# Seven block products in place of eight in the gelu half of two up-projections

## The chip, the cores and the metric

The kernel runs on one core of a Trainium2 chip. The metric is device time in microseconds (us) of one execution, and smaller is better. The core has a matrix engine (TensorE, PE in the profile; its weight loads are listed as PEld), a vector engine (VectorE, DVE), a scalar engine for activation functions and copies (ScalarE, ACT), a general engine (GpSimd, POOL) and an engine that mostly issues transfers (SyncE, SP). Each engine works through its own queue in order, and they meet by semaphores. Matmul results go to eight banks of an accumulator memory, each of 128 partitions by 512 fp32 columns; all other tiles lie in on-chip memory or in DRAM.

## The reference

Two decoder layers on x of 512 tokens by 1024 features: layer 0 mixes tokens by dilated attention, layer 1 by a gated linear recurrence, and each is followed by a gated convolutional feed-forward network. The change touches the feed-forward networks alone:

```python
def causal_dwconv(x, w, b):
    K = w.shape[0]
    S = x.shape[1]
    xp = jnp.pad(x, ((0, 0), (K - 1, 0), (0, 0)))
    out = b
    for k in range(K):
        out = out + xp[:, k:k + S] * w[k]
    return out

def conv_ffn(x, w_up, conv_w, conv_b, w_down):
    u = causal_dwconv(x @ w_up, conv_w, conv_b)
    g, v = u[..., :D_FF], u[..., D_FF:]
    return (jax.nn.gelu(g, approximate=True) * v) @ w_down
```

D_FF is 3072, the convolution has three taps along the tokens, and `x @ w_up` is 512 x 1024 by 1024 x 6144. Its first 3072 columns go through gelu (the gelu half), the others are multiplied onto them (the value half).

## The kernel before, in words

**Precision.** Matmuls take the fast fp32 format, which keeps fewer bits. So each operand is held as a rounded part hi and a remainder lo, and each product is three matmuls: hi by hi, hi by lo, lo by hi (`mm3`, L257, and `PASSES`, L255). `split` (L148) makes the two parts of a weight tile: ScalarE copies into hi (L149), VectorE subtracts hi from the raw tile into lo (L150).

**Activations.** A layer's normalized input lies transposed in two tiles hT (hi and lo), 128 partitions by 8 feature blocks by 512 tokens.

**Weights.** All weights are read in chunks of 1 MB in the order of the list `plan`. For an up-projection the plan alternates for j = 0 to 11: a gelu chunk (256 columns of the gelu half, all 1024 rows), then the value chunk with the same j. `load` (L193) issues a chunk's transfer on SyncE's queue into one of three raw buffers (RAW_BUFS). `parts_of` (L157) cuts a chunk into two units of 128 columns, and `pump` (L167) splits one unit per step into hi and lo, in two cuts of 512 columns each, as long as fewer than eight units live (W_UNITS). It asks for more chunks only when no cut piece is left over. `take` hands a unit to the matmuls, `done` gives it back, and `tick` (L222), called after each tile of matmuls, moves the side work on by a step and pumps one or two units. So the order on every engine follows from the places of these calls in the program: nothing is scheduled later.

**The up-projection.** `ffn` (L591) runs j = 0 to 11 and calls `feat_tiles(2, hT, ...)` (L433). For each of the two chunks and each of its two units it takes a bank and lets `feat` (L423) run 8 feature blocks by 3 passes, 24 matmuls of 128 x 128 weights by 512 tokens. Pair j = 0 runs in two halves of 256 tokens, since the last tokens' normalization comes late. After each tile the `sink` (L607) is issued: `conv` (L594) has ScalarE scale and bias the bank into a tile u (L596) and VectorE add the two other taps from the bank (L600, 511 and 510 columns). Gelu tiles (b = 0, 1) then go through gelu on ScalarE (L611) and stay until the down-projection; value tiles (b = 2, 3) are multiplied onto the gelu tiles by VectorE (L615).

**The rest.** `rows_proj` (L458) is the down-projection with the post-norm, which adds onto the residual x, held in `x_sb` (128 x 4 x 1024 fp32) for the whole program. Two `gain` buffers (128 x 1024) hold norm gains, and a pool of 32 tiles of 128 x 512 (`gen`) holds everything else. GpSimd's queue issues transfers of the attention, of gains and of transposed tiles; while an up-projection runs it has nothing to do.

## Time and profile before

| | |
|---|---|
| median time of 3 runs | 1455.94 us (1455.89 to 1456.03) |
| span of the profiled execution, first to last instruction | 1454.0 us (the page gives no time of its own for it) |
| mean granted TensorE clock | 0.999 |
| chain from pair 0 to the end of layer 0's up-projection | 1176 matmuls, 510.5 to 764.3 us |
| moved by transfers | 172.76 MB, mean 119 GB/s |

The profile is one execution. Busy time of an engine is the union of its instructions; a group row gives, for one line, engine and shape, the busy time, the mean length of one instruction in ns, and the idle time just before them with what ended it. Matmuls are pipelined: a row may say 390 ns for a matmul while the next starts after 227, so pitches are taken from long stretches and not from lengths. The chain that ended last is followed back from the last instruction through what released each step. A row of the windows gives, for a stretch, its length and then busy time and number of instructions of PE, PEld, DVE, ACT and POOL, then the granted clock, the transfers' share and GB/s.

### The profile page before, as it was taken

The numbers are of one execution on the slowest core, as the hardware profiler recorded it, in microseconds if no ns is written. First come the engines' busy times: TensorE is split into PE (matmuls) and PEld (weight loads), VectorE is DVE, ScalarE is ACT, GpSimd is POOL, SyncE is SP. The second block draws the span as 40 slices with busy tenths as digits, with TensorE's granted clock in tenths as the row PEclk, the third lists the DMA queues.
The fourth block names the chain that finished last, engine by engine and source line by source line (L and its number), as shares of the span: only waits on it lengthen the run. The fifth ranks groups of instructions, "written<-read, shape, count | busy, mean of one in ns | idle before, by whom it ended". The sixth has DMA issues, their size and how long they took to land.

```text
span 1454.0 us, 18793 instructions
## 1 busy us (share of the span) xinstructions
PE 1445.0 (99%) x6861; PEld 1214.4 (84%) x6861; DVE 879.8 (61%) x1955; ACT 675.9 (46%) x1532; POOL 133.9 (9%) x275
## 2 busy tenths in 40 slices
PE   9999999999999999999999999999999999999998
PEld 7888888888888898888888888888898888888886
DVE  6767747474735975555564338769775555564333
ACT  7656636262615553343444335589453434444221
POOL 0340414040402100000000001000100000000000
PEclk9999999999999999999999999999999999999999
DMA  7653637372726343323323322432333233223201
GB/s 225 207 146 109 174 113 208 104 215 97 216 96 211 102 131 100 103 87 102 101 88 116 115 73 88 131 116 84 120 102 116 87 102 102 87 104 128 88 0 58
DMA packets 125364, 172.76 MB, mean 119 GB/s; under 512 B 8736, under 2 KB 102392, under 8 KB 125272
## 3 DMA queue, kind: packets, MB, share of 16 engines
q1 hardware_dynamic: 114280, 145.48, 31.0%
q0 software_dynamic: 10144, 25.04, 5.9%
q8 instruction: 54, 0.88, 0.2%
q10 hardware_dynamic: 848, 1.05, 0.2%
q14 instruction: 38, 0.31, 0.1%
HBM read 156.24 MB, written 15.29 MB: 118 GB/s over the span
## 4 chain that ended last, share of the span: by engine, by line
PE 93%; ACT 4%; DVE 3%; issue 1%; DVEq 0%; ACTq 0%
PE ps L259 55%; PE acc L259 24%; PE v L758 8%; PE v L688 1%; DVE xb L967 1%; PE O L909 1%; PE S L854 1%; PE S L808 1%; DVE wlo L150 1%; ACT sig L988 1%; ACT whi L149 1%; PE O L259 1%; PE tr L341 1%; ACT sig L1007 0%; ACT a L1005 0%
## 5 line engine op out<-in xcount | busy, mean ns | idle before, releaser
L259 PE MATMUL ps<-hT,whi 128*128 128x512 f32 (+1 forms) x2752 | 801.3, 375 | 0.0
L259 PEld LDWEIGHTS ps<-hT,whi 128*128 128x128 f32 x2752 | 503.6, 188 | 91.6
L259 PE MATMUL ps<-hT,wlo 128*128 128x512 f32 (+1 forms) x1376 | 515.3, 374 | 0.0
L150 DVE TENSOR_TENSOR wlo<-raw,whi 128x512 fp32r<-128x512 f32 x360 | 230.8, 686 | 187.2 <-ACT whi L149 187.1
L259 PEld LDWEIGHTS ps<-hT,wlo 128*128 128x128 f32 x1376 | 259.1, 188 | 46.5
L149 ACT ACTIVATE whi<-raw 128x512 fp32r<-128x512 f32 x360 | 204.6, 621 | 135.4 <-PE acc L259 121.0
L600 DVE SCALAR_TENSOR_TENSOR u<-ps,cols,u 128x511 f32<-128x511 f32 x192 | 143.8, 749 | 140.6 <-ACT u L596 137.2
L259 PE MATMUL acc<-whi,ahi 128*128 128x512 f32 x512 | 199.7, 390 | 0.0
L259 PE MATMUL acc<-whi,alo 128*128 128x512 f32 x512 | 199.4, 389 | 0.1
L259 PE MATMUL acc<-wlo,ahi 128*128 128x512 f32 x512 | 199.3, 389 | 0.0
L143 ACT ACTIVATE whi<-raw,first_w 128x128 fp32r<-128x128 f32 (+1 forms) x432 | 146.2, 425 | 56.6 <-PE ps L259 33.9
L596 ACT ACTIVATE u<-ps,cols 128x512 f32<-128x512 f32 x96 | 74.8, 779 | 210.0 <-PE ps L259 210.0
L144 DVE SCALAR_TENSOR_TENSOR wlo<-raw,first_w,whi 128x128 fp32r<-128x128 f32 (+1 forms) x432 | 139.5, 389 | 1.4 <-ACT whi L143 1.3
L259 PEld LDWEIGHTS acc<-whi,alo 128*128 128x128 f32 x512 | 96.1, 188 | 20.5 <-DVE alo L150 0.5
L259 PEld LDWEIGHTS acc<-whi,ahi 128*128 128x128 f32 x512 | 96.1, 188 | 19.8
L259 PEld LDWEIGHTS acc<-wlo,ahi 128*128 128x128 f32 x512 | 96.2, 188 | 19.8
L758 PE MATMUL v<-whi,hT 128*128 128x512 f32 x320 | 102.4, 393 | 0.0
L302 POOL DMA_DIRECT2D turned<-T x36 | 19.6, 547 | 763.4 <-DVE T L296 759.9
L309 POOL DMA_DIRECT2D ft<-turned x144 | 78.7, 554 | 39.6 <-issue 17.7
L758 PEld LDWEIGHTS v<-whi,hT 128*128 128x128 f32 x320 | 60.1, 188 | 12.3
L611 ACT ACTIVATE u<-u 128x512 f32<-128x512 f32 x48 | 30.3, 632 | 80.4 <-DVE u L600 80.4
L758 PE MATMUL v<-wlo,hT 128*128 128x512 f32 x160 | 62.3, 389 | 0.0
(171 smaller groups left out, 1010.7 us busy)
## 6 DMA issues: line engine op xcount, KB each, us to landing
raw<-in_ffn_w_up_dram SPq DMA_DIRECT2D x48, 1024.0 KB
raw<-in_attn_w_qkv_dram SPq DMA_DIRECT2D x67, 512.0 KB
raw<-in_ffn_w_down_dram SPq DMA_DIRECT2D x24, 1024.0 KB
raw<-in_lru_w_in_dram SPq DMA_DIRECT2D x8, 1024.0 KB
turned<-T POOLq DMA_DIRECT2D x28, 256.0 KB, 2.6
ft<-turned POOLq DMA_DIRECT2D x112, 64.0 KB, 5.8
vrows<-v SPq DMA_DIRECT2D x16, 256.0 KB
vp<-vrows SPq DMA_DIRECT2D x16, 256.0 KB
```

The lines of the kernel that those rows point to most:

```text
L143: nc.scalar.activation(hi[:, k], raw[:, k], AF.Copy, scale=w)
L144: nc.vector.scalar_tensor_tensor(lo[:, k], raw[:, k], w, hi[:, k].bitcast(F32), op0=ALU.mult, op1=ALU.subtract)
L149: nc.scalar.activation(hi, raw, AF.Copy)
L150: nc.vector.tensor_tensor(lo, raw, hi.bitcast(F32), op=ALU.subtract)
L259: mm(dst, l[a], r[b], start=start and n == 0, stop=stop and n == 2)
L302: nc.gpsimd.dma_start(d, T)
L309: nc.gpsimd.dma_start(t[32 * c : 32 * c + 32].rearrange("j (b x) -> j b x", b=4), d.rearrange("(b j) (c x) -> c j b x", j=32, c=4)[c],)
L341: nc.tensor.transpose(ps[:, k * P : (k + 1) * P], xs[i][:, k * P : (k + 1) * P], ident)
L596: nc.scalar.activation(u, ps, AF.Identity, scale=cc[:, j : j + 1], bias=cc[:, 48 + j : 49 + j])
L600: nc.vector.scalar_tensor_tensor(u[:, d:], ps[:, : S - d], wc, u[:, d:], op0=ALU.mult, op1=ALU.add)
L611: nc.scalar.activation(u, u, AF.Gelu_apprx_tanh)
L758: mm(banks[t], hT[a][:, k, t * P : (t + 1) * P], W[b][:, k % 2, :], start=(k, a, b) == (0, 0, 0), stop=(k, a, b) == (KD - 1, 1, 0),)
```

## The change

For j = 3 to 10 in both layers (16 pairs) the gelu chunk's 256 x 1024 by 1024 x 512 product is done in 2 x 2 blocks: two halves of 128 output columns (m), two halves of 512 rows (k), two halves of 256 tokens (n). Seven block products (Strassen's scheme in Winograd's form) replace the eight, each of 4 feature blocks by 3 passes, 12 matmuls of 128 x 128 weights by 256 tokens.

*Weights* (`summed`). With a, b the two row halves of the first 128 columns and c, d of the other 128, c becomes c + d by a transfer on GpSimd's queue (`add_rows`, issued by `load` behind the chunk's own transfer), which reads d from DRAM a second time and adds it into the raw buffer. Four units follow in the raw buffer: (a, c+d); then VectorE makes a + c + d; (a + c + d, b); then VectorE makes two more sums; the third unit; and d alone. The first three are split in one piece of 1024 columns, d in one of 512. The pieces of a pair are ordered: value unit 0, the four gelu units, value unit 1. `pump` starts on a pair when both its chunks are asked for.

*Tokens* (`token_sums`). Once per layer, as side work from pair 1 on, GpSimd adds hi and lo of hT, VectorE forms four sums of its blocks, and they are split into hi and lo. They lie in the place of `x_sb`, in both gain buffers and in four pool tiles. For that, x is copied to DRAM first and comes back at j = 11 (`x_back`); `X[0]` names the tile that holds it now.

*Products* (`seven`). Numbers 1 to 7 are products, letters a to h are quarters of the value chunk's two tiles (6 matmuls of 512 tokens each). Bank y0 gathers products 1 and 2 in columns 0 to 255, bank y1 products 5, 3, 6, 7, 4. Between them ScalarE copies product 5 and then 5 + 3 out of y1 and writes minus product 1 into it, VectorE writes a difference into the other half of y0 after product 6 and of y1 after product 7. The four sinks are issued behind 2, d, 4 and h.

The diff, without the hunks that only rename `x_sb` to `X[0]`:

```diff
@@ -36,6 +36,7 @@
 TOE_BUFS = 2
 CP_PAD = 8
 WARM = 5
+SEVEN = range(3, 11)
 
 SHORT_ORDER = [
     ([0, 1], [0, 1, 2]), ([0], [3]), ([2, 3], [0]), ([1], [3]), ([2, 3], [1]), ([2], [2, 3]), ([3], [2, 3]),
@@ -153,6 +154,44 @@
     state = {"dma": 0, "cv": 0, "live": 0, "next": 0, "hold": False}
     raws, units, pieces = {}, {}, []
     sides, first_w, first_y, one = [], [], [], []
+
+    def plain(i, j, raw):
+
+        def f(hi, lo):
+            h = raw.shape[1] // 2
+            cuts = [(slice(None), slice(0, h)), (slice(None), slice(h, 2 * h))]
+            if raw.shape[1] == 1:
+                cuts = [(slice(None), slice(0, 1), slice(n, n + 512)) for n in (0, 512)]
+            if plan[i][4] is not None:
+                split_normed(hi, lo, raw, plan[i][4] + (2 * j if plan[i][0] == "value" else 0))
+                cuts = []
+            for c in cuts:
+                split(hi[c], lo[c], raw[c])
+
+        return (i, j), list(raw.shape[1:]), f
+
+    def summed(i, raw):
+
+        a, b, c, d = (raw[:, 4 * k : 4 * k + 4, m * P : m * P + P] for m, k in ((0, 0), (0, 1), (1, 0), (1, 1)))
+        shape = [KD, P]
+
+        def first(hi, lo):
+            two = [h.rearrange("p (k m) c -> p k (m c)", m=2) for h in (hi, lo)]
+            split(*two, raw[:, 0:4, :])
+            nc.vector.tensor_tensor(a, a, c, op=ALU.add)
+
+        def second(hi, lo):
+            split(hi, lo, raw[:, :, 0:P])
+            nc.vector.tensor_tensor(b, a, b, op=ALU.add)
+            nc.vector.tensor_tensor(a, a, d, op=ALU.subtract)
+
+        def third(hi, lo):
+            split(hi, lo, raw[:, :, 0:P])
+
+        def fourth(hi, lo):
+            split(hi[:, 0:4], lo[:, 0:4], d)
+
+        return [((i, n), shape, f) for n, f in enumerate((first, second, third, fourth))]
 
     def parts_of(kind, raw):
 
@@ -168,24 +207,21 @@
 
         for _ in range(limit):
             i = state["cv"]
-            if not pieces and i < state["dma"]:
-                pieces.extend((i, j, u) for j, u in enumerate(parts_of(plan[i][0], raws.pop(i))))
-                state["cv"] += 1
+            if not pieces and i + (i < len(plan) and plan[i][0] == "wino") < state["dma"]:
+                if plan[i][0] == "wino":
+                    u, v = summed(i, raws.pop(i)), [
+                        plain(i + 1, j, r) for j, r in enumerate(parts_of("feat", raws.pop(i + 1)))
+                    ]
+                    pieces.extend([v[0], *u, v[1]])
+                    state["cv"] += 2
+                else:
+                    pieces.extend(plain(i, j, r) for j, r in enumerate(parts_of(plan[i][0], raws.pop(i))))
+                    state["cv"] += 1
             if pieces and state["live"] < W_UNITS:
-                i, j, raw = pieces.pop(0)
-                hi, lo = (
-                    wp.tile([P] + list(raw.shape[1:]), F32R, tag=t, name=nm("w" + t)) for t in ("hi", "lo")
-                )
-                h = raw.shape[1] // 2
-                cuts = [(slice(None), slice(0, h)), (slice(None), slice(h, 2 * h))]
-                if raw.shape[1] == 1:
-                    cuts = [(slice(None), slice(0, 1), slice(n, n + 512)) for n in (0, 512)]
-                if plan[i][4] is not None:
-                    split_normed(hi, lo, raw, plan[i][4] + (2 * j if plan[i][0] == "value" else 0))
-                    cuts = []
-                for c in cuts:
-                    split(hi[c], lo[c], raw[c])
-                units[i, j] = (hi, lo)
+                key, shape, fill = pieces.pop(0)
+                hi, lo = (wp.tile([P] + shape, F32R, tag=t, name=nm("w" + t)) for t in ("hi", "lo"))
+                fill(hi, lo)
+                units[key] = (hi, lo)
                 state["live"] += 1
             while not pieces and state["dma"] < len(plan) and state["dma"] - state["cv"] < RAW_BUFS:
                 load()
@@ -198,8 +234,13 @@
         for src, n in srcs:
             nc.sync.dma_start(raw[:, :, at : at + n] if kind == "value" else raw[:, at : at + n, :], src)
             at += n
+        if kind == "wino":
+            add_rows(raw[:, 0:4, P:256], srcs[0][0][:, 4:8, P:256])
         raws[i] = raw
         state["dma"] += 1
+
+    def add_rows(to, src):
+        nc.gpsimd.dma_start(to, src, accum_op=ALU.add)
 
     def chunk():
         i = state["next"]
@@ -234,12 +275,12 @@
         while sides:
             tick()
 
-    def w_cols(w, c0, normed=False):
+    def w_cols(w, c0, normed=False, kind="feat"):
         if normed:
             srcs = [(w[i * 512 : (i + 1) * 512, c0 : c0 + 256].rearrange("(p k) c -> p k c", k=4), 4) for i in range(2)]
         else:
             srcs = [(w[:, c0 : c0 + 256].rearrange("(k p) c -> p k c", p=P), KD)]
-        plan.append(("feat", KD, 256, srcs, 0 if normed else None))
+        plan.append((kind, KD, 256, srcs, 0 if normed else None))
 
     def w_value(w, *cuts):
 
@@ -617,11 +658,140 @@
         order = [([0, 1, 2, 3], range(9)), ([0], range(9, 12)), ([1], range(9, 12))]
         order += [([2, 3], [9]), ([2], [10, 11]), ([3], [10, 11])]
         prep, run = rows_proj(12, act_split(gv), order, post, pre)
+        T = []
         for j in range(12):
+            if j == 1:
+                side(token_sums(hT, T))
             if j == 11:
+                x_back()
                 prep(3)
-            feat_tiles(2, hT, lambda b, ps: sink(b, ps, j), j == 0)
+            if j in SEVEN:
+                seven(hT, T, lambda b, ps: sink(b, ps, j))
+            else:
+                feat_tiles(2, hT, lambda b, ps: sink(b, ps, j), j == 0)
         return run()
+
+    kept = []
+
+    def x_back():
+
+        X[0] = cp.tile([P, 4, D], F32, tag="x_sb", name=nm("x_sb"))
+        nc.gpsimd.dma_start(X[0], kept.pop())
+
+    def token_sums(hT, T):
+
+        assert len(sides) == 1
+        d = dp.tile([P, 4, D], F32, name=nm("x_kept"))
+        nc.gpsimd.dma_start(d, X[0])
+        kept.append(d)
+        homes = cp.tile([P, 4, D], F32R, tag="x_sb", name=nm("T"))
+        homes = [homes[:, n] for n in range(4)]
+        homes += [cp.tile([P, D], F32R, tag="gain", name=nm("T"), bufs=2) for _ in range(2)]
+        homes = [[h[:, 0:512], h[:, 512:1024]] for h in homes]
+        homes += [[gen(F32R, "T") for _ in range(2)] for _ in range(2)]
+        homes = [[h.rearrange("p (k t) -> p k t", k=2) for h in hs] for hs in homes]
+        yield 1
+
+        def both(k0, n):
+            o = gen(s="B").rearrange("p (k t) -> p k t", k=2)
+            hi, lo = (h[:, k0 : k0 + 2, n * 256 : n * 256 + 256] for h in hT)
+            nc.gpsimd.tensor_tensor(o, hi.bitcast(F32), lo.bitcast(F32), op=ALU.add)
+            return o
+
+        tt = nc.vector.tensor_tensor
+        B = {}
+        for k in range(2):
+            for n, at in (((0, 0), 2 * k), ((0, 1), 2 * k), ((1, 1), 4 + 2 * k), ((1, 0), 4 + 2 * k)):
+                B[k, n] = both(at, n[1])
+        yield 2
+        for k in range(2):
+            b11, b12, b22, b21 = (B[k, n] for n in ((0, 0), (0, 1), (1, 1), (1, 0)))
+            tt(b11, b11, b12, op=ALU.subtract)
+            tt(b12, b12, b22, op=ALU.subtract)
+            tt(b22, b22, b11, op=ALU.add)
+            tt(b21, b21, b22, op=ALU.subtract)
+            yield 1
+            for n, b in enumerate((b11, b22, b12, b21)):
+                split(homes[2 * n][k], homes[2 * n + 1][k], b)
+            if not k:
+                yield 1
+        T.extend([homes[2 * n], homes[2 * n + 1]] for n in range(4))
+
+    def seven(hT, T, sink):
+
+        i, iv = chunk(), chunk()
+        t = gen(s="part")
+        y, v = {}, {}
+
+        def block(kr, n):
+            return lambda h, k: hT[h][:, 4 * kr + k, n * 256 : n * 256 + 256]
+
+        def turn(n):
+            return lambda h, k: T[n][h][k // 2][:, k % 2]
+
+        def pairs(m):
+            return lambda w, k: w.rearrange("p (k m) c -> p k m c", m=2)[:, k, m]
+
+        def row(k0):
+            return lambda w, k: w[:, k0 + k]
+
+        left = {
+            1: (0, pairs(0), block(0, 0), 0), 5: (0, pairs(1), turn(0), 1), 6: (1, row(0), turn(1), 1),
+            2: (1, row(4), block(1, 0), 0), 7: (2, row(0), turn(2), 1), 3: (2, row(4), block(1, 1), 1),
+            4: (3, row(0), turn(3), 1),
+        }
+
+        def product(n):
+            u, l, r, b = left[n]
+            W = take(i, u)
+            if b not in y:
+                y[b] = psum()
+            for k in range(4):
+                for q, (wa, ha) in enumerate(PASSES):
+                    mm(
+                        y[b][:, 0:256], l(W[wa], k), r(ha, k), start=n in (1, 5) and k == q == 0,
+                        stop=k == 3 and q == 2, skip_group_check=True,
+                    )
+
+        def quarter(n):
+            m, k0 = n // 4, 2 * (n % 4)
+            W = take(iv, m)
+            if m not in v:
+                v[m] = psum()
+            for k in (k0, k0 + 1):
+                mm3(v[m], [w[:, k, :] for w in W], [h[:, k, :] for h in hT], k == 0, k == KD - 1)
+
+        a, c = (lambda: y[0][:, 0:256]), (lambda: y[1][:, 0:256])
+        p5, z = t[:, 0:256], t[:, 256:512]
+        for step in "5a13bc62d7ef4gh":
+            if step in "1234567":
+                n = int(step)
+                product(n)
+                if n == 5:
+                    nc.scalar.activation(p5, c(), AF.Copy)
+                elif n == 1:
+                    done()
+                elif n == 3:
+                    nc.scalar.activation(z, c(), AF.Copy)
+                    nc.scalar.activation(c(), a(), AF.Copy, scale=-1.0)
+                elif n == 6:
+                    nc.vector.tensor_tensor(y[0][:, 256:512], z, c(), op=ALU.subtract)
+                elif n == 2:
+                    done()
+                    sink(0, y[0])
+                elif n == 7:
+                    done()
+                    nc.vector.tensor_tensor(y[1][:, 256:512], c(), p5, op=ALU.subtract)
+                else:
+                    done()
+                    sink(1, y[1])
+            else:
+                n = "abcdefgh".index(step)
+                quarter(n)
+                if n % 4 == 3:
+                    done()
+                    sink(2 + n // 4, v[n // 4])
+            tick()
 
 
     def attention(hT, post, pre):
@@ -1072,7 +1242,7 @@
             for c in range(4):
                 w_rows(lru_w_out[0], c * 256)
         for j in range(12):
-            w_cols(ffn_w_up[layer], j * 256)
+            w_cols(ffn_w_up[layer], j * 256, kind="wino" if j in SEVEN else "feat")
             w_cols(ffn_w_up[layer], D_FF + j * 256)
         for c in range(12):
             w_rows(ffn_w_down[layer], c * 256)
```

More of the change, by code (lines that the diff above doesn't have):

```diff
@@ L130 @@
     make_identity(nc, ident)
-    x_sb = cp.tile([P, 4, D], F32, tag="x_sb", name="x_sb")
+    X = [cp.tile([P, 4, D], F32, tag="x_sb", name="x_sb")]
     def gain(src, layer, eng=nc.gpsimd):
@@ L315, in prenorm @@
     def prenorm(t, hT, g, wait):
-        xh, gh = halves(x_sb[:, t, :]), halves(g)
+        xh, gh = halves(X[0][:, t, :]), halves(g)
         xs = [gen(s="xs") for _ in range(2)]
@@ L353, in first_transposed @@
                 ps[:, k % 4 * P : (k % 4 + 1) * P],
-                x_sb[:, t, i * 512 : i * 512 + 512].rearrange("t (p k) -> t k p", k=4)[:, k % 4], ident,
+                X[0][:, t, i * 512 : i * 512 + 512].rearrange("t (p k) -> t k p", k=4)[:, k % 4], ident,
             )
@@ L375, in first_squares @@
             nc.scalar.activation(
-                junk, x_sb[:, t, i * 512 : i * 512 + 512], AF.Square, accum_out=first_ss[i][:, t : t + 1]
+                junk, X[0][:, t, i * 512 : i * 512 + 512], AF.Square, accum_out=first_ss[i][:, t : t + 1]
             )
@@ L409, in postnorm @@
         for i, c in enumerate(at):
-            xc = x_sb[:, t, c]
+            xc = X[0][:, t, c]
             nc.vector.scalar_tensor_tensor(xc, u[i], y, xc, op0=ALU.mult, op1=ALU.add)
@@ L1090, in x_half @@
         c = slice(i * 512, (i + 1) * 512)
-        nc.sync.dma_start(x_sb[:, t, c], x[0, t * P : (t + 1) * P, c])
+        nc.sync.dma_start(X[0][:, t, c], x[0, t * P : (t + 1) * P, c])
     def w_part(i, k0, k1):
```

## The prediction

> **What bounds the kernel now.** First the page's list of engines, then the share of the chain that ended last:
>
> ```profile
> span 1454.0 us, 18793 instructions
> PE 1445.0 (99%) x6861; PEld 1214.4 (84%) x6861; DVE 879.8 (61%) x1955; ACT 675.9 (46%) x1532; POOL 133.9 (9%) x275
> PE 93%; ACT 4%; DVE 3%; issue 1%; DVEq 0%; ACTq 0%
> ```
>
> TensorE is busy for 99% of the span and carries 93% of the chain, so a cheaper set of matmuls is the right place to look. How close it runs shows in the chain in order of time, asked from 495 to 900 us (start, length, what); that stretch holds all of layer 0's up-projection:
>
> ```profile
> 500.13 5.75 PE ps L259 x48
> 510.50 253.77 PE ps L259 x1176
> 764.27 125.12 PE acc L259 x552
> ```
>
> The first row is 48 matmuls of 256 columns (the halves of pair 0): 5.75/48 = 0.1198 us each. The last is 552 of 512 columns: 0.2267 us each. Between them 1176 matmuls run with nothing else in the chain: in the up-projection TensorE waits for nobody. A pair j (gelu chunk and value chunk, 96 matmuls of 512) lasts 96 x 0.2267 = 21.76 us. What the other engines do meanwhile, over eight pairs (busy time and count by engine):
>
> ```profile
> 568.00:742.00 174.00, 174.00 (x769) 144.12 (x769) 98.98 (x144) 68.41 (x112) 0.00 (x0) 1.00 0.29 97
> ```
>
> VectorE (third engine) works 12.4 us a pair, ScalarE (fourth) 8.6, GpSimd nothing. They have room, but only because nothing on TensorE hangs on them soon: a finished tile sits in its bank while 5.4 us of the next tile run, and weights are split up to eight units ahead.
>
> **What the change takes away.** A gelu chunk was 48 matmuls of 512, 48 x 0.2267 = 10.88 us. Seven products of 4 x 3 matmuls of 256 are 84 x 0.1198 = 10.06 us. So 0.82 us a pair, 16 pairs: 13.1 us, or 0.9%. The saving is so much less than one eighth because a 256-column matmul costs 53% of a 512-column one.
>
> The Trainium skill ("TensorE: Matmul & The Clock Gate", Back-to-back issue gap) gives columns/2.4 + 2.5 ns. By it the saving would be 48 x 215.8 - 84 x 109.2 ns = 1.19 us a pair, 19 us in all; the rows above are of this very work, so I go by them.
>
> **What it adds on VectorE and ScalarE.** Durations (mean ns, second number behind the bar), from the groups by line with shapes kept apart:
>
> ```profile
> L150 DVE TENSOR_TENSOR wlo<-raw,whi 128x512 fp32r<-128x512 f32 x360 | 230.8, 686 | 187.2 <-ACT whi L149 187.1
> L149 ACT ACTIVATE whi<-raw 128x512 fp32r<-128x512 f32 x360 | 204.6, 621 | 135.4 <-PE acc L259 121.0 <-PE ps L259 14.4
> L143 ACT ACTIVATE whi<-raw,first_w 128x128 fp32r<-128x128 f32 x384 | 115.2, 390 | 24.1 <-PE ps L259 24.1
> L143 ACT ACTIVATE whi<-raw,first_w 128x512 fp32r<-128x512 f32 x48 | 31.4, 713 | 32.5 <-DMA raw<-in_attn_w_qkv_dram 22.7 <-PE ps L259 9.9
> L144 DVE SCALAR_TENSOR_TENSOR wlo<-raw,first_w,whi 128x128 fp32r<-128x128 f32 x384 | 105.8, 345 | 1.3 <-ACT whi L143 1.3
> L144 DVE SCALAR_TENSOR_TENSOR wlo<-raw,first_w,whi 128x512 fp32r<-128x512 f32 x48 | 33.7, 744 | 0.1
> L596 ACT ACTIVATE u<-ps,cols 128x512 f32<-128x512 f32 x96 | 74.8, 779 | 210.0 <-PE ps L259 210.0
> L600 DVE SCALAR_TENSOR_TENSOR u<-ps,cols,u 128x511 f32<-128x511 f32 x96 | 71.9, 749 | 137.2 <-ACT u L596 137.2
> L600 DVE SCALAR_TENSOR_TENSOR u<-ps,cols,u 128x510 f32<-128x510 f32 x96 | 71.9, 749 | 3.4
> L615 DVE TENSOR_TENSOR u<-u,u 128x512 f32<-128x512 f32 x48 | 33.2, 692 | 1.6
> L611 ACT ACTIVATE u<-u 128x512 f32<-128x512 f32 x48 | 30.3, 632 | 80.4 <-DVE u L600 80.4
> ```
>
> No row has 1024 or 256 columns of this kind, so I scale. ScalarE: (713-390)/384 = 0.84 ns a column; a 1024-wide split is 0.621 + 0.43 = 1.05 us (bounds: one 512 row, 0.62, and two of them, 1.24), a 256-wide copy 0.41 (bounds 0.39 and 0.62). VectorE: (744-345)/384 = 1.04 ns a column; 1024 wide is 1.22 (0.69 to 1.37), 256 wide 0.42 (0.34 to 0.69).
>
> Per pair VectorE loses four 512 subtractions (2.74) and gains three 1024 subtractions (3.66), one of 512, three weight sums of 512 (2.74 together) and two 256 differences in the banks (0.84): 12.4 + 4.5 = 16.9 us. ScalarE loses 2.48 and gains 3.15 + 0.62 + 1.23: about 11.1. Both still fit in 21 us. As a sum, then, all of it hides. It does not hide as a chain, because TensorE now waits for these engines inside the pair. Its order is 5 a 1 3 b c 6 2 d 7 e f 4 g h; a product takes 12 x 0.1198 = 1.44 us, a value quarter 6 x 0.2267 = 1.36. Three waits are new.
>
> *Before product 4.* It adds to bank y1, from which VectorE must first have taken product 7's difference. VectorE's queue is in order, and between the end of product 2 and that difference stand: ScalarE's first tap of gelu tile 0 (0.78), two taps on VectorE (1.50), gelu (0.63, ahead of the next split on ScalarE), the third weight unit's split (1.05) and subtraction (1.22), the two taps of value tile 0 (1.50), its multiply (0.69), the fourth unit's subtraction (0.69), and the difference (0.42). Sum 8.5 us. TensorE has d, 7, e and f to cover it: 1.44 + 3 x 1.36 = 5.5. It stands for about **3.0 us**. Behind product 4 in TensorE's queue are g, h and the next pair, so nothing fills the hole. With the low bounds of the scaled items the stand is 1.9, with the high ones 3.6.
>
> *Before product 2.* VectorE's difference after product 6 goes into columns 256 to 511 of bank y0, product 2 into 0 to 255 of the same bank, with nothing between 6 and 2. If product 2 waits, it waits for the last matmul of 6 to drain, the difference (0.42), and what VectorE still has ahead (two weight sums of 0.69 each, partly beside product 6). How long a drain is:
>
> ```profile
> L259 PE MATMUL ps<-hT,whi 128*128 128x256 f32 x384 | 69.9, 284 | 0.0
> L259 PEld LDWEIGHTS ps<-hT,whi 128*128 128x128 f32 x2752 | 503.6, 188 | 91.6
> ```
>
> 0.28 us per matmul less the 0.12 pitch is 0.16; with two handovers and the difference 0.65, with a late VectorE up to 1.3. I take **0.8**. Whether it waits at all no row shows, since the kernel before never lets VectorE write a bank in use. The Trainium skill ("PSUM — Partial Sum Buffer", PSUM bank collisions raise a hardware error) says two engines must be kept apart by bank, not by address. If columns alone counted, this term would be nothing and the time 13 us shorter.
>
> *Before product 6.* ScalarE must copy y1 out and write minus product 1 into it. From the end of product 4: tap 0.78, taps 1.50, gelu 0.63, two value splits 1.24, tap of value tile 1 0.78, taps 1.50, multiply 0.69, first unit's subtraction 1.22 and sum 0.69, second unit's split 1.05, two copies 0.82: 10.9 us. TensorE has g, h, 5, a, 1, 3, b, c: 5 x 1.36 + 3 x 1.44 = 11.1. An even race: I take **0.3** (0 to 0.8).
>
> **What hides.** A gelu chunk's load is asked for a whole pair ahead (three raw buffers, a pair takes two), and the adding transfer follows it on GpSimd's queue, which is otherwise idle here. Rows for its size, last number the us from issue to landing:
>
> ```profile
> turned<-T POOLq DMA_DIRECT2D x28, 256.0 KB, 2.6
> cn<-crow POOLq DMA_DIRECT2D x8, 256.0 KB, 6.1
> gain<-in_norm_ffn_post_dram POOLq DMA_DIRECT2D x2, 512.0 KB, 4.0
> ```
>
> A load of 1 MB (some 4 to 8 us by the last row) and an addition of 2.6 to 6.1 are done 10 to 20 us before the first split wants them; beyond that each us would cost ScalarE one, in every pair. The token sums (per layer 8 sums on GpSimd, 8 on VectorE, 8 splits: 11 us of VectorE, 5 of ScalarE) fall into pairs 1 and 2, where both are idle for over a third; the first seven-product pair starts with their backlog, 2 us a layer (0 to 8, since no row has a GpSimd sum). The copy of x out and back has the whole projection and GpSimd's queue to itself: nothing. SyncE's loads go out in twos instead of singly, after the pair's last piece; they keep over half a pair of lead.
>
> **Sum.** Stands 3.0 + 0.8 + 0.3 = 4.1 a pair, less 0.82: +3.3 us, 16 pairs +52.5; backlog 2 x 2 = 4; and TensorE's restart after 48 stands, whose next weight load is no longer hidden (0.19 at most, its row's mean; say 0.04 each): 2. Together +58 on a span of 1454.0: 1512. The runs shown have a median of 1455.94, 1.9 above that span, which I carry over: **1514 us**. With all low bounds a pair gains 1.9 + 0.65 - 0.82 = 1.7 us (+28, 1484), with all high ones 3.6 + 1.3 + 0.8 - 0.82 = 4.9 and 16 of backlog (+94, 1550).
>
> **Rivals.**
> *Slower still, by late sums.* GpSimd's token sums or the adding transfers take some three times what I allow; the first pairs of each layer, or ScalarE in each pair, wait for them. For it: no row shows either operation. Against: the long lead. Some 20 us more: 1535. Chance 9%.
> *The clock falls in the stands.* The last matmul in the timeline (start, length), and the clock column (before the last two) after it:
>
> ```profile
> 1446.93 0.39 PE L259 MATMUL acc<-whi,alo 128*128 128x512 f32 x1
> ...
> 1451.00:1452.00 1.00, 0.00 (x0) 0.00 (x0) 0.00 (x0) 0.00 (x0) 0.00 (x0) 1.00 0.99 371
> 1452.00:1453.00 1.00, 0.00 (x0) 0.00 (x0) 0.00 (x0) 0.00 (x0) 0.00 (x0) 0.77 0.41 154
> ```
>
> The matmul ends at 1447.3; the clock was still whole after 4.7 us of rest. If a stand of 3 us halved it until product 5, then 4, g and h (4.16 us) would take twice that: 67 us more, 1581. Chance 3%. The Trainium skill (the TensorE page above, Part 1) wants an idle window of about 3.4 us, free-running, before the clock drops; by it a 3.0 us stand never does it, a 3.6 us one seldom.
> *Milder.* The wide operations lie at their low ends and product 2 does not wait: a pair costs 1 us: 1475. Chance 4%.
> *Not slower.* The difference before product 4 comes in time. Only if the chain from product 2 to it is at most 5.7 us instead of 8.5 (5.5 of cover, and 0.15 beside the 0.65 at product 2) do the stands eat no more than the 0.82 saved. With no stand at all the time is 1456 - 13 = 1443. For it: VectorE and ScalarE are not full. Against: eight of its ten items are rows as they stand. Chance 3%.
> *The blocks cost TensorE more.* Were 256-column products with changing weights bound by weight loads, a pair would lose; but pair 0's halves load new weights for each matmul at 0.1198. 1%, 1550.
>
> Forecast 80%, own range 1490 to 1540. The range for all, 1488 to 1550, leaves out the clock, the milder case and the gain. A measurement of this kernel can tell about 0.2% from no change: faster 3%, same 1%, slower 96%.
>
> **What would show it.** In the profile after: TensorE no longer at 99% but near 95%, products waiting for VectorE (some 3 us, then 0.8, once a pair each) with ScalarE third and small; pairs 3 to 10 lasting about 25 us instead of 21.76; a 256-column pitch near 0.12; no wait on the adding transfer; the clock whole. I would be wrong if products follow each other without gaps, if the gaps stand at DMA, or if a 1024-wide operation differs much from 1.05 and 1.22 us.

## The result and the profile after

| | before | after |
|---|---|---|
| median time | 1455.91 us (1455.77 to 1456.03, 4 runs) | 1555.55 us (1554.24 to 1556.32, 4 runs) |
| span of the profiled execution | 1454.0 us | 1554.5 us |
| mean granted TensorE clock | 0.999 | 0.979 |

The ratio is 1.0684 (95% interval 1.0669 to 1.0699): 100 us slower, where the prediction had 58 and a range of 32 to 94. The page's list of engines and the first lines of the chain that ended last:

```profile
span 1554.5 us, 20305 instructions
PE 1466.9 (94%) x7437; PEld 1247.5 (80%) x7437; DVE 989.1 (64%) x2067; ACT 718.1 (46%) x1596; POOL 176.8 (11%) x311
PE 71%; DVE 17%; ACT 7%; issue 2%; DMA 2%; DVEq 0%; ACTq 0%
```

TensorE's share of the chain went from 93% to 71%, and VectorE's from 3% to 17%. Although fewer columns are multiplied, TensorE is busy 22 us longer: a sign of a lower clock. The stages of layer 0 stand in the chain in order of time (start, length, what):

```profile
501.41 5.75 PE ps L300 x48
...
815.66 84.55 PE acc L300 x373
```

From pair 0 to the down-projection it takes 815.66 - 501.41 = 314.25 us, against 764.27 - 500.13 = 264.14 before: 50.1 us more. Layer 1, reckoned alike, has 49.1 us more, and the stretch ahead of the up-projections 1.3. Pair by pair (the windows, each from one product 5 to the next; pairs 3, 4, 5 and 9; columns length, PE, PEld, DVE, ACT, POOL, clock, transfers):

```profile
569.50:610.00 40.50, 27.00 (x133) 23.09 (x133) 30.75 (x44) 19.30 (x33) 1.33 (x1) 0.79 0.34 98
610.00:636.60 26.60, 23.05 (x133) 20.18 (x132) 16.82 (x24) 11.22 (x19) 1.29 (x1) 0.94 0.33 92
636.60:661.70 25.10, 21.56 (x134) 18.98 (x134) 16.62 (x23) 9.47 (x16) 1.27 (x1) 1.00 0.28 73
...
740.10:766.90 26.80, 23.14 (x133) 20.23 (x132) 16.63 (x23) 11.42 (x19) 0.00 (x0) 0.94 0.29 96
```

Three kinds of pair can be read off the length and the clock. Pairs at full clock (5 and 8) take 25.0 to 25.1 us, 3.3 more than the 21.76 of before; that is the forecast figure, in part by luck (see the restart, below). Pairs at 0.94 (4, 6, 7 and 9) take 26.6 to 26.8, another 1.7. And pair 3 takes 40.5 us at a mean clock of 0.79. So the 50.1 us of layer 0 are 18.7 in pair 3 and 31.4 in the other seven, which is 7 x 3.3 and five falls of the clock (pair 10 has one, too) at 1.7. The prediction lacks two things: what happened in pair 3, and the falls. The waits of TensorE (in all, times, longest):

```profile
PE ps L751 <- DVE ps L784: 47.7, 16, 3.2
PE ps L751 <- ACT T L150: 13.0, 4, 6.1
PE ps L751 <- DVE ps L778: 10.1, 16, 0.7
PE ps L751 <- DVE T L151: 7.6, 4, 3.6
PE ps L751 <- ACT ps L776: 0.6, 1, 0.6
```

L784 is the difference before product 4: 47.7/16 = 2.98 us a pair. L778 is the one before product 2: 0.63. L776, before product 6, is nearly nil. These three are the prediction's new waits. Waits on T, the token sums, stand in pair 3 alone: 20.6 us in both layers.

**Where pair 3's time starts.** Some 22 us before, in pair 1, VectorE's and GpSimd's rows of the timeline (start, length):

```profile
547.01 11.82 DVE L151 TENSOR_TENSOR wlo<-raw,whi 128x1024 fp32r<-128x1024 f32 x1
547.23 10.51 POOL L698 TENSOR_TENSOR B<-hT,hT 128x512 f32<-128x512 f32 x8
```

One subtraction of 1024 columns took 11.82 us. It ended 1.1 us after the last of GpSimd's eight sums, about the time that it takes alone: it looks as if it got nothing done until they were through. In layer 1 the same two rows have 11.86 and 10.48 us. All other subtractions of that size take 1.22: VectorE did one instruction in 11.8 us and came some 10.6 us behind.

**Where the clock falls.** The stand in pair 3 before product 4, cut where the clock changes:

```profile
601.19:604.60 3.41, 0.46 (x4) 0.40 (x4) 3.34 (x6) 0.81 (x2) 0.00 (x0) 1.00 0.00 0
604.60:608.01 3.41, 3.41 (x15) 3.12 (x15) 1.05 (x3) 0.78 (x1) 0.00 (x0) 0.50 0.90 291
...
652.39:655.80 3.41, 2.05 (x9) 1.34 (x8) 2.74 (x4) 2.80 (x5) 0.00 (x0) 1.00 0.00 0
655.80:659.21 3.41, 1.82 (x14) 1.78 (x15) 2.73 (x5) 0.09 (x1) 0.00 (x0) 1.00 0.26 61
```

All falls of this execution start a whole number of 3.41 us apart. In the window up to 604.60 TensorE was busy for 0.46 us, and the clock is half in the next. In pair 5 a stand of the same length lies across the border at 655.80, each window keeps 1.8 us of work or more, and the clock stays whole (pair 5's row above has 1.00). In both up-projections together it is at half speed for 61.4 us, half of that in the two pairs 3 (17.1 and 13.7 us).

### The profile page after: what moved, and what is told of

It reads as the page before. It is cut to its first block, busy times and chain, and to the rows that moved or that the text cites. A ratio compares the mean times of both kernels' runs of the same rounds, so it can differ in the third digit from the quotient of the medians.

```text
span 1554.5 us, 20305 instructions
## 1 busy us (share of the span) xinstructions
PE 1466.9 (94%) x7437; PEld 1247.5 (80%) x7437; DVE 989.1 (64%) x2067; ACT 718.1 (46%) x1596; POOL 176.8 (11%) x311
## 3 DMA queue, kind: packets, MB, share of 16 engines
q1 hardware_dynamic: 114280, 145.48, 29.4%
## 4 chain that ended last, share of the span: by engine, by line
PE 71%; DVE 17%; ACT 7%; issue 2%; DMA 2%; DVEq 0%; ACTq 0%
PE ps L300 28%; PE acc L300 22%; PE ps L751 7%; PE v L928 7%; DVE wlo L151 7%; DVE u L641 5%; ACT whi L150 2%; DMA raw<-in_ffn_w_up_dram 2%; PE v L858 2%; DVE xb L1137 1%; ACT u L637 1%; ACT u L652 1%; PE O L1079 1%; PE S L1024 1%; PE S L978 1%
## 5 line engine op out<-in xcount | busy, mean ns | idle before, releaser
L300 PE MATMUL ps<-hT,whi 128*128 128x512 f32 (+1 forms) x2240 | 656.6, 378 | 0.0
L300 PEld LDWEIGHTS ps<-hT,whi 128*128 128x128 f32 x2240 | 409.9, 192 | 68.8
L300 PE MATMUL ps<-hT,wlo 128*128 128x512 f32 (+1 forms) x1120 | 420.4, 375 | 0.0
L151 DVE TENSOR_TENSOR wlo<-raw,whi 128x512 fp32r<-128x512 f32 (+1 forms) x360 | 280.4, 817 | 215.1 <-ACT whi L150 215.0
L150 ACT ACTIVATE whi<-raw 128x512 fp32r<-128x512 f32 (+1 forms) x360 | 226.9, 679 | 219.6 <-PE acc L300 124.7
L300 PEld LDWEIGHTS ps<-hT,wlo 128*128 128x128 f32 x1120 | 214.5, 192 | 38.7
L641 DVE SCALAR_TENSOR_TENSOR u<-ps,cols,u 128x511 f32<-128x511 f32 x192 | 143.5, 747 | 84.5 <-ACT u L637 81.0
L751 PE MATMUL ps<-T,whi 128*128 128x256 f32 x512 | 102.6, 297 | 69.0 <-DVE ps L784 47.7
L751 PEld LDWEIGHTS ps<-T,whi 128*128 128x128 f32 x512 | 85.5, 198 | 82.7 <-DVE ps L784 54.5
L300 PEld LDWEIGHTS acc<-whi,alo 128*128 128x128 f32 x512 | 96.1, 188 | 20.6 <-DVE alo L151 0.5
L751 PE MATMUL ps<-hT,whi 128*128 128x256 f32 x384 | 72.8, 289 | 10.1 <-DVE ps L778 10.1
```

The costliest lines, as they stand in the source:

```text
L150: nc.scalar.activation(hi, raw, AF.Copy)
L151: nc.vector.tensor_tensor(lo, raw, hi.bitcast(F32), op=ALU.subtract)
L300: mm(dst, l[a], r[b], start=start and n == 0, stop=stop and n == 2)
L641: nc.vector.scalar_tensor_tensor(u[:, d:], ps[:, : S - d], wc, u[:, d:], op0=ALU.mult, op1=ALU.add)
L751: mm(y[b][:, 0:256], l(W[wa], k), r(ha, k), start=n in (1, 5) and k == q == 0, stop=k == 3 and q == 2, skip_group_check=True,)
```

## The experiments

Three theories were put against each other. A: GpSimd's sums shut VectorE out, and pair 3 pays. B: the stands make the clock fall, at some 1.6 us a time. C: everything hangs on where the side work stands in the order, not on its amount. The rival to all: the chains before products 4 and 2 are simply longer than reckoned. Where a run is compared with the changed kernel (1555.55 us), both stand against the same kernel before, 1455.8 to 1455.9.

**e1_sums_vector.** The eight token sums on VectorE, nothing else:

```diff
-            nc.gpsimd.tensor_tensor(o, hi.bitcast(F32), lo.bitcast(F32), op=ALU.add)
+            nc.vector.tensor_tensor(o, hi.bitcast(F32), lo.bitcast(F32), op=ALU.add)
```

> The eight sums of hi and lo per layer move from GpSimd to VectorE, nothing else. Theory A (GpSimd's sums keep VectorE from its own two-input work, so one subtraction of 1.22 us took 11.8): that subtraction is back at 1.2 us, the first product of pair 3 waits under 3 us in all instead of some 11, the clock stays whole there, and the time falls by 20 to 30 us, to about 1530, although VectorE has 5.5 us a layer more to do. Rival (the token sums are simply issued too late and too long, whoever does them): VectorE gets 5.5 us more, pair 3 still waits about as long, the time changes by less than 5 us.

Measured 1535.56 us (ratio 1.0549, 1.0535 to 1.0564), 20.0 less, though VectorE has 16 sums of 0.69 us more to do. Its group of the 1024-column subtraction, and the waits:

```profile
L151 DVE TENSOR_TENSOR wlo<-raw,whi 128x1024 fp32r<-128x1024 f32 x48 | 58.7, 1223 | 40.6 <-ACT whi L150 40.5
```

```profile
PE ps L751 <- DVE ps L784: 47.7, 16, 3.2
...
PE ps L751 <- DVE T L151: 2.5, 2, 1.4
```

The mean is 1.223 us with no outlier (1.665 in the changed kernel), and the waits on T fall from 20.6 to 2.5 us. The stands before product 4 are the same to the digit. A holds, and moving the sums is worth 20 us. Two things are to be added. The clock does not stay whole in pair 3: it falls twice there in each layer, against the expectation, and a new wait before product 6 appears (3.7 us in two times). And the edit does more than free VectorE: the sums now begin at 538.6 us instead of 547.2, since on GpSimd they stood in its queue behind an adding transfer, and they take 4.9 us instead of 10.5. The changed kernel's own rows say how little that explains (an estimate from them): the first differences need four of the sums, which were done by about 547.2 + 4 x 1.31 = 552.5 us, and VectorE's queue came to these differences at 561.6, or at 551.0 without the 10.6 us lost; it would have found each sum done in time.

**e2_sums_alone.** No seven-product pair; the sums and the copies of x stay, and what they make is not read:

```diff
-SEVEN = range(3, 11)
+SEVEN = range(0)
```

> No pair uses seven products; the token sums and the copies of x to DRAM and back stay, and nothing reads the token sums. Theory A: VectorE stands about 10.5 us in both layers here too, but a plain pair has eight units and free banks ahead, so TensorE waits 0 to 5 us a layer and the time is 1456 to 1466. Rival (the sums and copies cost by themselves, wherever they stand): some 15 us a layer, 1485.

Measured 1457.02 us (ratio 1.0008, 0.9999 to 1.0018). VectorE and GpSimd compete here as well (timeline):

```profile
512.19 11.51 POOL L698 TENSOR_TENSOR B<-hT,hT 128x512 f32<-128x512 f32 x7 [3.94 <-DVE hT L387]
512.63 9.91 DVE L151 TENSOR_TENSOR wlo<-raw,whi 128x512 fp32r<-128x512 f32 x6
```

Six subtractions that take 0.69 us each elsewhere took 9.91. So VectorE lost 5.8 us here, not the 10.5 expected, and at an earlier place. All the same the time grows by 1.2 us only: with eight-product pairs TensorE needs nothing of it soon. Such a loss costs where a matmul is due behind it, not by itself.

**e3_fill.** Twelve matmuls of 256 columns without a use, into the dead half of a bank, ahead of product 4 in all 16 pairs:

```diff
             if step in "1234567":
                 n = int(step)
+                if n == 4:
+                    for q in range(12):
+                        mm(y[0][:, 0:256], hT[0][:, q % 8, 0:P], hT[0][:, q % 8, 0:256], start=True, stop=True)
                 product(n)
```

> Twelve useless matmuls of 256 columns (1.44 us of TensorE) go into the dead half of bank y0 right ahead of product 4 in each of the 16 pairs; the rest is as in the changed kernel. Theory B (the clock falls because TensorE rests over 3 us ahead of product 4): the rest shrinks to about 1.6 us, the granted clock is 1.00 in pairs 4 to 10, and a kernel with 192 more matmuls is 15 to 20 us faster, about 1537. Rival (the clock falls for another reason, as the load of all engines): the clock falls as often, the time stays within 3 us or grows.

Measured 1544.26 us (ratio 1.0606, 1.0592 to 1.0621): 192 more matmuls, and 11.3 us less. Half-clock time is 30.7 us, in pairs 3 and 10 alone. The window of pair 6, and two around the fall in pair 10:

```profile
657.50:682.80 25.30, 23.06 (x146) 20.48 (x145) 16.63 (x23) 10.77 (x18) 1.27 (x1) 1.00 0.35 94
```

```profile
777.68:781.09 3.41, 1.64 (x13) 1.44 (x13) 3.37 (x6) 1.25 (x3) 0.00 (x0) 1.00 0.95 239
781.09:784.50 3.41, 3.41 (x16) 3.12 (x15) 1.04 (x3) 0.78 (x1) 0.00 (x0) 0.50 0.98 366
```

A pair with its clock whole costs 25.3 us, 0.2 to 0.3 more than an undisturbed pair of the changed kernel, since the fill is not quite hidden. B holds: work that fills the hole keeps the clock up. Half of the 61.4 us at half speed go, worth 15, and the 0.2 to 0.3 us in 16 pairs take some 4 back. The expectation had pair 10 at a whole clock, too; its fall shows that here 1.64 us of work in a window of 3.41 did not suffice.

**e5_both.** The sums on VectorE as in e1, and the side work re-placed: the weight pieces are split one at a time at six named places (P; the expectation of e4 below counts nine), each sink is parted into its taps (t) and its gelu or multiply (e), and quarter d goes ahead of product 2:

```diff
-        for step in "5a13bc62d7ef4gh":
+        for step in "5 a 1 P 3 P b c 6 P d t2 2 t0 7 e0 e2 P e f P 4 t1 P g e1 h t3 e3".split():
...
+            elif step == "P":
+                pump(1)
```

> The same work as in the changed kernel, but token sums on VectorE, and the side work of a pair issued at other places: each weight piece right behind a copy or difference that TensorE waits for and never ahead of one, value tile 0's last quarter between products 6 and 2, gelu and multiply behind product 7's difference. Theory C (the stands are queue order on VectorE and ScalarE, not too much work): no stands from pair 4 on, a pair of 20.9 us, the clock whole, and a time of 1443 to 1452, faster than the kernel before. Rival (VectorE's added work is the bound, 16.9 us a pair and its waits): pairs of 24 us or more, time over 1490.

Measured 1451.04 us (ratio 0.9968, 0.9955 to 0.998): faster than before. Pairs 3 and 4:

```profile
568.30:592.80 24.50, 21.83 (x134) 19.05 (x133) 20.63 (x31) 11.47 (x19) 1.31 (x1) 1.00 0.40 108
592.80:613.80 21.00, 21.00 (x134) 18.94 (x133) 16.27 (x23) 10.92 (x17) 1.28 (x1) 1.00 0.36 101
```

Only pair 3 still waits, 2.7 us. In pair 4 VectorE works 16.3 us, as it did in the changed kernel (16.6 to 16.8), and TensorE stands no longer: the 21.0 us are 0.8 less than 21.76, the saving that the prediction reckoned. C holds.

**e4_moved.** The order of e5, but the sums left on GpSimd.

> Side work re-placed as in e5_both (weight splits one piece at a time at nine named places, the taps of a sink apart from its gelu or multiply), but the eight token sums stay on GpSimd. Theory (two separate causes): from pair 4 on TensorE no longer stands and the clock stays whole, pairs of about 21 us; but the first seven-product pair of each layer still waits 10 us or more for the token sums, because VectorE is still shut out while GpSimd adds; so some 20 us above e5_both (1451), 1465 to 1480. If the stands alone were the cause: within 5 us of e5_both. If the re-placing did nothing and the sums on VectorE were what helped: about 1555.

Measured 1471.67 us (ratio 1.0108, 1.0094 to 1.0122), 20.6 above e5. Pairs 3 and 4 again:

```profile
569.50:603.50 34.00, 24.22 (x133) 21.20 (x134) 29.70 (x43) 18.62 (x32) 1.33 (x1) 0.80 0.29 78
603.50:624.50 21.00, 21.00 (x134) 18.94 (x133) 16.26 (x23) 10.92 (x17) 1.28 (x1) 1.00 0.37 102
```

Pair 3 costs 34.0 us instead of 24.5, the others nothing; the waits left in the up-projections are those on T, 20.8 us in all. The two causes are apart and add up: the sums' place is worth 20.0 us with the stands (e1) and 20.6 without them; the order is worth 83.9 with the sums on GpSimd and 84.5 without.

**e6_order.** Quarter d between products 6 and 2:

```diff
-        for step in "5a13bc62d7ef4gh":
+        for step in "5a13bc6d27ef4gh":
```

The value tile's sink, due behind d, is put off until product 2's sink is issued.

> Only the order of the products changes: quarter d goes between products 6 and 2 (the value tile's sink stays behind product 2). If product 2 waited for VectorE's difference in the other half of its bank, d's 1.36 us now cover it: the wait on that line (0.7 us in each of 16 pairs) vanishes, and with one quarter less between 2 and 4 that quarter's time is lost again before product 4 unless the chain there starts earlier too. Forecast: wait at product 2 nil, stand before product 4 from 3.1 to between 3.1 and 4.5 us, half-clock windows as many or more; 1535 to 1565. If the 0.8 us were not a matter of the bank: the wait stays and the time is 1555.

Measured 1547.61 us (ratio 1.0636, 1.0621 to 1.065). The first of the waits and the last that concerns a product (between them those on T), and a window that ends in a fall:

```profile
PE ps L752 <- DVE ps L785: 47.7, 16, 3.5
...
PE ps L752 <- ACT ps L777: 1.0, 2, 0.5
```

```profile
652.90:656.30 3.40, 1.40 (x11) 1.40 (x12) 3.11 (x6) 0.27 (x1) 0.00 (x0) 1.00 0.18 36
656.40:659.80 3.40, 3.40 (x10) 2.72 (x9) 1.50 (x2) 1.41 (x3) 0.00 (x0) 0.50 1.03 334
```

The row for the difference before product 2 is gone: that wait was for VectorE's write into the other half of the bank, and 1.36 us of other work hide it. The stand before 4 stays 47.7/16. But in the profiled execution, the slowest of the four (1552.26 us), the clock falls in all 16 pairs (half for 88.7 us). That takes back 13.7 us. With its fall, a pair behind pair 3 lasts 25.4 to 25.9 us; without the 1.7 it would be some 1.1 us shorter than the 25.0 of an undisturbed pair of the changed kernel, more than the wait of 0.63.

**e7_chain.** No weight piece is split in the two steps behind product 2 and quarter d:

```diff
+            state["hold"] = step in "2d"
             tick()
+            state["hold"] = False
```

> Order as in e6_order, and no weight piece is split in the steps behind product 2 and quarter d; those pieces come later. That takes 1.05 + 1.22 + 0.69 us of other work out of the chain between product 2 and the difference before product 4. If that chain is what my sum says (8.5 us), the stand before product 4 falls from 3.1 us to 0.2 to 1; the delayed pieces then make product 6 wait for ScalarE's two copies, up to 2 us. Stands this short halve the clock seldom: half-clock time well below 61 us. 1515 to 1540. If instead the taps alone set the stand: it stays at 3 us, 1555.

(The expectation is mistaken in one thing: the order of products in this kernel is that of the changed kernel, not of e6_order, so the wait before product 2 was bound to stay.) Measured 1532.42 us (ratio 1.0526, 1.0512 to 1.054). The waits:

```profile
PE ps L752 <- ACT part L772: 16.3, 12, 1.5
PE ps L752 <- DVE ps L785: 15.0, 16, 0.9
...
PE ps L752 <- ACT ps L777: 4.0, 12, 0.3
```

The stand before 4 falls from 2.98 to 0.94 us: the chain is what the prediction wrote down, and its foreign items are the splits. They turn up again 1.4 us a time, not before product 6 as expected but before product 3, which waits until ScalarE has copied product 5 out of the bank (L772). With stands of 1.5 us and less the clock falls in pair 3 alone (half for 27.3 us), and that is most of the gain, 17 of 23 us. A pair at a whole clock is no shorter than before, 25.2 to 25.4 us against 25.0:

```profile
656.61:681.98 25.37, 21.98 (x133) 18.90 (x132) 16.55 (x24) 10.73 (x17) 1.27 (x1) 1.00 0.34 93
```

The long stand was cut into shorter ones, not removed.

**e9_own_sum.** The changed kernel with the first weight sum on VectorE, without the adding transfer:

```diff
-        if kind == "wino":
-            add_rows(raw[:, 0:4, P:256], srcs[0][0][:, 4:8, P:256])
...
+            nc.vector.tensor_tensor(c, c, d, op=ALU.add)
             split(*two, raw[:, 0:4, :])
```

> The changed kernel with its first weight sum made by VectorE just before the first unit's split, in place of the adding transfer. The transfers land 4.5 us after their issue and no product waits for them, so theory: they cost nothing, and the sum's 0.7 us on VectorE come on top: the chain before product 6 (10.9 against 11.1 us of cover) is now 0.5 us late, the stands before 2 and 4 stay (0.7 and 3.1): 5 to 12 us slower than the changed kernel, 1558 to 1570, with the changes that another fall of the clock makes (1.6 us each). If the adding transfer held the first split up: faster than 1555.

Measured 1579.2 us (ratio 1.0845, 1.083 to 1.086): 23.7 slower than the changed kernel, twice what was expected. The sum (L179) in pair 6's chain, and the new wait:

```profile
668.37 0.69 DVE raw L179
...
669.09 1.06 ACT whi L150
670.14 0.28 ACT part L770
...
670.47 1.70 PE ps L750 x12
```

```profile
PE ps L750 <- ACT part L770: 18.2, 12, 2.2
```

The sum takes 0.69 us, but it stands in VectorE's queue behind the taps and the multiply of the value tile. ScalarE holds the first split back for it, and with the split the copy of product 5, for which product 3 waits. So it is again product 3, not 6, by 1.5 us in 12 pairs; half-clock time rises to 78.5 us. The adding transfer itself cost nothing that was waited for, and it spared this.

**e8_fourteen.** e5 with seven products for j = 4 to 10 and the step after the sums one tick shorter:

```diff
-SEVEN = range(3, 11)
+SEVEN = range(4, 11)
...
-        yield 2
+        yield 1
```

> e5_both with seven products for j = 4 to 10 only (14 pairs instead of 16) and the step from the sums to the differences one tick earlier. The token sums then have a pair more before they are needed. Theory: the stands left in e5_both (3.2 us in the first such pair of each layer) vanish, worth 6 us, and the two pairs that go back to eight products cost 2 x 0.75: 1444 to 1449, half clock nowhere. If those stands were due to something other than late sums: 1451 to 1453.

Measured 1446.64 us (ratio 0.9941, 0.9928 to 0.9955): the fastest. The page's engines (span 1444.6 us), and one window over all seven-product pairs of layer 0 and nearly all of the eight-product pair behind them:

```profile
PE 1435.2 (99%) x7365; PEld 1227.4 (85%) x7365; DVE 968.1 (67%) x2073; ACT 717.0 (50%) x1590; POOL 154.1 (11%) x293
```

```profile
590.40:758.00 167.60, 167.60 (x1017) 149.77 (x1016) 129.68 (x183) 87.47 (x140) 8.05 (x8) 1.00 0.44 134
```

TensorE is busy in every us of the stretch. The gain of 9.1 us compares with 14 x 0.82 = 11.5 saved; the sums and copies by themselves cost 1.2 (e2), and the last 1.2 are open.

**e10_fourteen_own.** e8 with e9's replacement of the adding transfer.

> The same replacement in e8_fourteen. VectorE then works some 17.6 us of a pair of 21, and no chain is closer than the weight splits' own lead. Theory (the sum hides as long as its place in the order does): within 3 us of 1446.6, no half clock. If VectorE's order is too full: stands return, 1450 to 1465. If the adding transfers cost transfers of weights anything: 1443 or less.

Measured 1450.93 us (ratio 0.9967, 0.9955 to 0.9979), 4.3 above e8: beyond the 3 that the first theory allowed, and at the low end of what the second gave. 3.6 us of waits for VectorE's two differences return: before product 2 in the first seven-product pair of each layer, before product 4 in two later pairs of layer 1. The clock stays whole. With the better order a sum on VectorE costs 4.3 us over 14 pairs, where it cost 23.7 over 16 in e9.

## Why the prediction was wrong, step by step

The sign and the mechanism of the larger part were right; the size was not.

- **The saving**, 0.82 us a pair: right. A product runs 12 matmuls in 1.42 us, and undisturbed pairs in e5 and e8 take 20.9 to 21.0 us for 21.76.
- **Before product 4**, 3.0 us: right (2.98), and by the chain written down (eleven operations, not ten; three of them scaled, and they came within 0.02 us). Pair 5's piece of the chain in order of time shows it item by item, from product 2 to the difference (L784):

```profile
647.20 1.72 PE ps L751 x12
...
648.94 0.79 ACT u L637
...
651.38 0.63 ACT u L652
652.01 0.96 ACT whi L150
...
653.00 1.22 DVE wlo L151
...
656.31 0.68 DVE wlo L151
656.99 0.03 DVE ps L784
```

- **Before product 2**, 0.8: right within 0.2 (0.63). By e6 product 2 waited for the difference, which writes other columns of its bank. The wait is one for a semaphore of the program; what the chip would do without it no run tells.
- **Before product 6**, 0.3: it hardly came (0.6 us in all). But e7 and e9 show that the tighter race on ScalarE was product 3's, for the copy of product 5, which the prediction had not looked at.
- **The restart after a stand, 0.04 us, 2 in all**: too small. In pair 5 the last matmul before product 4 starts at 654.05 us and the next at 657.39, a wait of 2.95; with the pitch of 0.23 and the slower first step (0.34 for two matmuls instead of 0.24) a stand costs 0.26 us beyond its wait. Two of them a pair are 0.5, over 16 pairs 8. The waits came to 3.65 a pair instead of 4.1, and so the two misses cancel to the 3.3 forecast: that agreement is luck.
- **The token sums' backlog, "2 us a layer (0 to 8, since no row has a GpSimd sum)"**: this step failed. Pair 3 took 18.7 us more instead of 3.3 and 2, and moving the sums off GpSimd gave back 20 us, both layers together. The length of the sums was not what was missing: eight took 10.51 us. What was: GpSimd and VectorE were reckoned as independent, "both are idle for over a third". While GpSimd read two tiles to add them, VectorE's instruction with two tiles of the same memory did not move. The Trainium skill ("SBUF — State Buffer", Who interferes with whom) says that a VectorE instruction with two inputs from this memory contends with a GpSimd instruction that reads it, that the shared ports are an exclusive lock, and that issue order decides who blocks. The trace agrees on the lock (11.82 us instead of 1.22, through all eight sums); it does not show the order, as VectorE's row begins 0.22 us before the first sum and still lost. The rival "late sums" had this size (20 us, 9%), by another mechanism.
- **The clock, 3%, 67 us**: this failed too, in both parts. It falls, in nine pairs besides the two pairs 3 of the profiled execution, and a fall costs about 1.7 us, because only one window of 3.41 us runs at half speed. What misled was the end of the kernel before, read as 4.7 us of rest at a whole clock. By the windows of the same trace, cut from the fall there (1452.54 us):

```profile
1445.71:1449.13 3.42, 1.61 (x8) 0.99 (x6) 1.92 (x7) 1.67 (x5) 0.00 (x0) 1.00 0.38 140
1449.13:1452.54 3.41, 0.00 (x0) 0.00 (x0) 1.61 (x4) 0.00 (x0) 0.00 (x0) 1.00 0.41 154
1452.54:1454.00 1.46, 0.00 (x0) 0.00 (x0) 0.00 (x0) 0.00 (x0) 0.00 (x0) 0.50 0.00 0
```

  The first 1.8 us of that rest lay in a window in which TensorE had still worked for 1.6. The next was empty, and the clock fell at its end. The Trainium skill ("TensorE: Matmul & The Clock Gate", Part 1) has the free-running window of 3.4 us and asks for an idle one; the trace agrees on the window, and not on idle. By that rule a stand of 3.0 us could not do it, and the chance was set at 3%.
- **What hides**: the adding transfers did (4.5 us from issue to landing, no wait on them), except that GpSimd's sums stood in the queue behind one. The loads have less lead than claimed: the transfer of the value chunk stands in the chain, since its buffer comes free only with the fourth unit's subtraction; no matmul waited on it directly.

In numbers, a layer was forecast at 8 x 3.3 + 2 + 1 = 29.4 us and took 50.1 (layer 0). 13.4 of the 20.7 missing are pair 3, 8.5 the five other falls; all the rest agrees to about 1 us, with the luck just named.

## What to carry to other kernels

When work moves to GpSimd, look up what VectorE runs in the same us: two engines with room each by their rows can be one engine where both read two operands from on-chip memory, and the price is paid where the first matmul depends on what comes behind. A stand of TensorE cost its length, 0.3 us of restart and, where more than half of a 3.4 us window was empty, another 1.7 us. And when engines have room as a sum but stands appear, take the chain apart first: here the same work in another order, with the sums on VectorE, turned a loss of 100 us into a gain of 5, and with one pair a layer left out, of 9.

## What the runs showed of the hardware

- **About half a window decides the clock.** In the up-projections of the changed kernel, e1, e3, e6, e7 and e9, each window of 3.41 us at full clock with TensorE busy for up to 1.58 us was followed by one at half speed, and none with 1.66 or more. Between the two it went both ways: after 1.64 and 1.65 in e3 it fell, after 1.61 to 1.63 in e1, 1.61 in e9, 1.64 in the changed kernel and 1.61 at the end of the kernel before it did not. Busy time includes modelled ends of matmuls, which count for more where matmuls run one by one: in e4 the clock fell after a window with 1.94 us, in which matmuls with waits between them are counted at 0.38 us each. So the border is near 1.6 us of matmuls in a row, just under half. From these figures one can estimate that a single stand below 1.7 us costs no clock, and that up to twice that it depends on where the stand lies.
- **Shut out, or turn by turn.** In e2 a 512-column subtraction and a GpSimd sum took turns, 1.70 us apart; in the changed kernel a 1024-column one got no turn for eight sums, though its row begins 0.2 us before theirs. Whether the width or the moment of the start decides, no run here tells.
- **GpSimd's sum of two 512-column tiles** takes 1.31 us (eight in 10.51; 1.64 in e2, where they took turns), against 0.69 for VectorE.
